# One Trainium2 core, a two-layer hybrid decoder trunk: group A's weights in four transfers, memory's products later, the first norm weighted on rows

## The chip, the cores and the metric

The kernel runs on one core of a Trainium2 chip. The core has TensorE (PE), VectorE (DVE), ScalarE (ACT), GpSimd (POOL) and SyncE (SP), which here only issues transfers. The metric is the device time of one execution in microseconds; lower is better. Times are compared as medians of several executions on the same chip.

## The reference, cut to what matters

The trunk has two layers over 256 tokens of width 1024, in fp32. Each layer normalises the tokens, projects them once, feeds five groups of heads, and projects their outputs back:

```python
for layer in range(DEPTH):
    h = rms_norm(x, pre_norm[layer])
    proj = jnp.einsum('bsd,de->bse', h, w_in[layer])          # 1024 x 8224
    (a_q, a_kv, a_gate, a_z, b_xbc, b_dt, b_z, c_q, c_kv, c_z,
     d_q, d_kv, d_z, m_q, m_z) = jnp.split(proj, offsets, axis=-1)
    a_out = nsa_mixer(...)         # A: compressed, selected and window branches, gated
    b_out = ssd_mixer(...)         # B: conv, Mamba-2 scan; dt = softplus(dt_raw + dt_bias)
    c_out, _ = banded_attention(rope(c_q), rope(c_k), ...)    # C: window 128, sinks
    d_out = dilated_mixer(...)     # D: three dilated windows
    m_out = memory_attention(m_q, mem, m_norm[layer], m_w_kv[layer])   # M: 256 memory tokens
    mix = jnp.concatenate([a_out * silu(a_z), b_out, c_out * silu(c_z),
                           d_out * silu(d_z), m_out * silu(m_z)], axis=-1)
    x = x + rms_norm(jnp.einsum('bse,ed->bsd', mix, w_out[layer]), post_norm[layer])
```

`rms_norm(x, w)` is `x * rsqrt(mean(x*x) + eps) * w`. `rms_norm(mem, m_norm)` is projected to keys and values inside `memory_attention`.

## The kernel before, in words

**Products in three parts.** fp32 accuracy is made from rounded operands: a weight block is loaded into a raw buffer R (`w_load`), rounded into H by a copy on ScalarE or VectorE, and the remainder is put into L by a subtraction on VectorE (`w_split`). The tokens, normalised and transposed, are kept in `hT_hi` and `hT_lo`. A product is then hi x hi, hi x lo and lo x hi. `fm` makes 128 output columns as feature rows for all 256 tokens from one load of 512 KB and 24 matmuls; `tm` makes token rows, by blocks of the contracted dimension (`ks`), 48 matmuls. There are five R buffers, four H and four L, 48 pages of 128x544 (P), and eight PSUM banks (B).

**Order.** Nothing runs as it is called. Every operation is recorded with its engines and estimated costs (`add`), and gets a key: the sum of the PE costs recorded so far plus an offset. `schedule` then simulates the engines: an engine that is free takes the ready operation with the lowest key. The order it finds is the program; each engine executes its own list in order, and semaphores hold the data dependences. The model's times are not waited for, only its order counts. Constants shape the keys: weight loads are due `DMA_EARLY` ahead of their products, splits `W_EARLY` ahead, attention units recorded by `bg` are due `BG_LATE` after, the two norms at the layers' edges are `URGENT`. A load by `dma` goes to SP's queue, at 450 ns of SP in the model; only rounded copies from elsewhere go to POOL's.

**Head (`setup`, `norm_transpose`).** PE first runs `N_WARM` filler products of a page of ones. SP loads the tokens in four parts, the constants (with the identity for transposes) and the norm weights, 32 rows of 128, which PE transposes to per-partition scalars `nw`. For each token tile t, ScalarE sums squares, VectorE makes the inverse root in small steps (`rsqrt`: a bit trick and three Newton steps of two operations), and the rows are scaled. PE transposes them; for each of eight 128-column blocks one operation multiplies by `nw` into `hT_hi` and one VectorE operation multiplies again and subtracts into `hT_lo`. The same function normalises memory (for both layers at once, with the second layer's result stored to DRAM) and the tokens of layer 1.

**Layer (`layer`).** In layer 0 memory's own query and gate products come first (`m_own`); then group A's two compressed key/value products, a `tm` of 288 columns (A's values, A's gates and B's `dt` columns, from three places of the weight, in blocks of 3, 3 and 2 of the eight 128-row blocks: nine transfers), `gates` (A's gates and B's step sizes: softplus of dt by a series, on 128x16 tiles), memory's key/value products and attention units (`m_rest`, `mem_kv`), A's remaining keys with the eight compression pieces, the queries and units of A; then D, B, C and the output products. The rope tables (`setup_rope`: a chain on VectorE and one sine on ScalarE) are recorded at the start with a key `ROPE_LATE` later. In the output products `LAST` of the 18 row blocks are held back, so that they can be done for the first token tile and then the second; the post-norm of the first tile then overlaps the second's products.

## Time and profile before

| | |
|---|---|
| median of 3 runs | 676.24 us (673.43 to 677.6) |
| profiled execution, its own time | 677.86 us |
| its span, first to last instruction | 676.1 us |
| mean granted TensorE clock | 0.991 |
| PE, DVE, ACT, POOL busy in the span | 658.2, 593.4, 474.1, 23.4 us |
| moved by DMA | 125.84 MB, mean 186 GB/s |

The span leaves out what lies around the first and the last instruction, 1.8 us here. Busy times of engines overlap. In the rows below, "L457 MATMUL" is the helper `mm`, "L463" the transpose, "L469" every ScalarE activation, "L486", "L491" and "L511" VectorE's two-tensor, one-tensor and fused operations, "L537" every DMA; tile names stand with their buffer numbers left out.

### The profile page before, as it was taken

Reading aid. Unit: us, or ns where it says so; the run is one execution under the profiler, and the core shown is the slowest. Engines: PE = TensorE matmul, PEld = TensorE weight load, DVE = VectorE, ACT = ScalarE, POOL = GpSimd, SP = SyncE. Lnnn points to the kernel's source line nnn. Section 1 sums busy time; section 2 is a strip of 40 time slices with the busy share of each in tenths; the row PEclk is TensorE's granted clock in tenths of the full one; section 3 lists DMA queues with packets and bytes.
Section 4 is the critical chain, followed back from the end, with each engine's and each line's share of the span. In section 5 each row is a group of like instructions: output and inputs, shape, how many; then the busy total and the mean of one; then the engine's idle time right before and its main releaser. Section 6 shows DMA issues by size and latency. Waiting matters only on the chain.

```text
span 676.1 us, 14725 instructions
## 1 busy us (share of the span) xinstructions
PE 658.2 (97%) x5043; PEld 625.7 (93%) x5043; DVE 593.4 (88%) x1754; ACT 474.1 (70%) x1180; POOL 23.4 (3%) x74
## 2 busy tenths in 40 slices
PE   8989998999999999999999999999999999999995
PEld 7979998999999999988889999999999999998884
DVE  6777989999978999989787879999898899998875
ACT  6663879996765878665475458998576677868541
POOL 3000000000000200100000000000000000000000
PEclk9979998999999999999999999999999999999999
DMA  7899574589998757664438958487989734776511
GB/s 212 226 298 293 164 187 112 153 218 244 236 247 212 185 146 217 184 196 143 158 108 224 258 135 213 104 224 197 237 213 245 199 87 120 208 211 176 156 36 62
DMA packets 177618, 125.84 MB, mean 186 GB/s; under 512 B 11510, under 2 KB 168840, under 8 KB 177544
## 3 DMA queue, kind: packets, MB, share of 16 engines
q1 hardware_dynamic: 176392, 122.81, 67.9%
q0 software_dynamic: 1152, 2.10, 1.2%
q8 instruction: 40, 0.66, 0.4%
q14 instruction: 34, 0.28, 0.1%
HBM read 110.14 MB, written 3.20 MB: 168 GB/s over the span
## 4 chain that ended last, share of the span: by engine, by line
PE 67%; DVE 14%; ACT 7%; DMA 5%; SPq 4%; issue 2%; DVEq 0%; ACTq 0%
PE B L457 64%; ACT P L469 6%; DVE P L486 4%; SPq L537 4%; DMA R<-in_w_in_dram 3%; PE B L463 3%; DVE L L486 3%; DVE P L511 2%; DVE P L515 2%; DVE S L511 1%; DMA P<-in_mem_dram 1%; ACT H L469 1%; DVE P L491 1%; DMA P<-scr 1%; DVE x L511 0%
## 5 line engine op out<-in xcount | busy, mean ns | idle before, releaser
L486 DVE TENSOR_TENSOR L<-R,H 128x1024 fp32r<-128x1024 f32 (+1 forms) x174 | 209.8, 1210 | 33.9 <-ACT H L469 30.9
L469 ACT ACTIVATE H<-R 128x1024 fp32r<-128x1024 f32 (+2 forms) x156 | 163.3, 1055 | 77.5 <-PE B L457 48.8
L469 ACT ACTIVATE P<-B 64x256 f32<-64x256 f32 (+10 forms) x364 | 143.7, 408 | 65.1 <-PE B L457 46.9
L469 ACT ACTIVATE P<-P,S 128x128 f32<-128x128 f32 (+5 forms) x256 | 111.3, 453 | 33.9 <-DVE S L524 17.1
L457 PE MATMUL B<-hT_hi,L 128*128 128x256 f32 x864 | 128.3, 285 | 3.3 <-DVE L L486 3.2
L457 PE MATMUL B<-P,P 128*128 128x256 f32 (+6 forms) x896 | 125.2, 280 | 0.4 <-ACT P L469 0.2
L457 PE MATMUL B<-hT_hi,H 128*128 128x256 f32 x864 | 123.8, 282 | 1.0 <-ACT H L469 1.0
L457 PE MATMUL B<-hT_lo,H 128*128 128x256 f32 x864 | 124.0, 282 | 0.0
L457 PEld LDWEIGHTS B<-P,P 128*128 128x128 f32 (+1 forms) x896 | 113.4, 184 | 3.7 <-DVE P L486 0.9
L457 PEld LDWEIGHTS B<-hT_hi,L 128*128 128x128 f32 x864 | 112.3, 190 | 4.2 <-DVE L L486 3.8
L457 PEld LDWEIGHTS B<-hT_hi,H 128*128 128x128 f32 x864 | 110.9, 188 | 2.3 <-ACT H L469 1.3
L457 PEld LDWEIGHTS B<-hT_lo,H 128*128 128x128 f32 x864 | 110.5, 188 | 0.2
L457 PE MATMUL B<-H,P 128*128 128x512 f32 (+1 forms) x352 | 102.8, 376 | 0.0
L486 DVE TENSOR_TENSOR P<-B,P 64x256 f32<-64x256 f32 (+5 forms) x186 | 92.3, 510 | 11.2 <-ACT P L469 8.8
L457 PEld LDWEIGHTS B<-H,P 128*128 128x128 f32 x352 | 62.1, 189 | 9.6
L457 PE MATMUL B<-L,P 128*128 128x512 f32 (+1 forms) x176 | 65.7, 373 | 0.0
L515 DVE CUSTOM_DVE_ANT_0 P<-B,P 128x128 f32<-128x128 f32 (+2 forms) x192 | 53.1, 320 | 0.4
L463 PE MATMUL B<-cst,P 128*128 128x128 f32 (+1 forms) x344 | 48.5, 275 | 1.2 <-DVE P L491 1.0
L457 PE MATMUL B<-H,hT_hi 128*128 128x256 f32 (+1 forms) x160 | 45.8, 286 | 0.0
L457 PE MATMUL B<-H,hT_lo 128*128 128x256 f32 (+1 forms) x160 | 45.4, 284 | 0.0
L457 PE MATMUL B<-L,hT_hi 128*128 128x256 f32 (+1 forms) x160 | 45.3, 283 | 0.0
L463 PEld LDWEIGHTS B<-cst,P 128*128 128x128 f32 (+1 forms) x344 | 38.4, 136 | 5.7 <-DVE P L491 1.4
(127 smaller groups left out, 665.1 us busy)
## 6 DMA issues: line engine op xcount, KB each, us to landing
R<-in_w_in_dram SPq DMA_DIRECT2D x124, 512.0 KB, 5.4
R<-in_w_out_dram SPq DMA_DIRECT2D x36, 512.0 KB, 3.9
P<-P SPq DMA_DIRECT2D x176, 64.0 KB, 3.9
P<-scr SPq DMA_DIRECT2D x64, 136.0 KB, 4.5
R<-in_m_w_kv_dram SPq DMA_DIRECT2D x8, 512.0 KB, 5.2
P<-in_a_cmp_w_dram SPq DMA_DIRECT2D x16, 256.0 KB, 5.3
mem_d<-P SPq DMA_DIRECT2D x8, 256.0 KB, 5.6
P<-mem_d POOLq DMA_DIRECT2D x8, 256.0 KB, 4.6
```

The costliest lines, as they stand in the source:

```text
L457: f = lambda: self.nc.tensor.matmul(out=out.ap(), lhsT=lhsT.ap(), rhs=rhs.ap(), start=start, stop=stop)
L463: f = lambda: self.nc.tensor.transpose(out.ap(), in_.ap(), idn.ap())
L469: f = lambda: self.nc.scalar.activation(out=out.ap(), in_=in_.ap(), func=func, **{k: _ap(x) for k, x in kw.items()})
L486: f = lambda: self.nc.vector.tensor_tensor(out=out.ap(), in0=a.ap(), in1=b.ap(), op=op)
L491: return lambda: eng.tensor_scalar(out.ap(), a.ap(), _ap(s1), _ap(s2), **kw)
L511: f = lambda: self.nc.vector.scalar_tensor_tensor(out=out.ap(), in0=a.ap(), scalar=_ap(s), in1=b.ap(), op0=op0, op1=op1)
L515: f = lambda: self.nc.vector.tensor_tensor_reduce(out=out.ap(), in0=a.ap(), in1=b.ap(), scale=1.0, scalar=3e38, op0=OP.add, op1=OP.min, ac ...
L537: f = lambda: eng.dma_start(out=_ap(out), in_=_ap(in_))
```

## The change

It does these things:

- The first norm of layer 0 is a new function, `norm_x`. The weight row is loaded into a zeroed buffer, and two fp32 products with a matrix of ones spread it over all partitions in PSUM. For the first token tile the rows are multiplied by the weight and later by the inverse root, for the second both at once. Each of four 512-column pieces is transposed into a bank of its own and split by two 512-wide operations.
- The constants are loaded in two parts, the identity first; the per-partition norm weights, now wanted by memory and layer 1 only, come later.
- Group A's `tm` has 280 columns from two places in blocks of 4 and 4: four transfers; R, H and L grow to 1120 columns. B's `dt` columns are loaded with the neighbouring first half of B's z (264 columns), and the step sizes are computed by `steps`, recorded in B. B's z products now come ahead of its x products.
- `m_rest` of layer 0 is recorded after A's remaining keys and six compression pieces, and memory's load and norm are due 12 instead of 6 us ahead of it.
- The model: SP has eight transfers in flight and costs 520 ns a turn, a PE operation is planned 800 ns after a result of another engine that it uses. Constants: `ROPE_LATE` 80 to 120 us, `LAST` 3 to 4, `N_WARM` 34 to 16 and others.
- `rsqrt` of one column has five steps instead of six.

```diff
...
 TW = 272
+WIDE = 1120
...
 N_RAW, N_HI, N_PAGES, N_SMALL = 5, 4, 48, 64
-SP_HORIZON = 30000.0
-HORIZON, BG_LATE, URGENT, ROPE, LAST = 80000.0, 15000.0, 20000.0, 8000.0, 3
+SP_HORIZON = 40000.0
+HORIZON, BG_LATE, URGENT, ROPE, LAST = 80000.0, 12000.0, 20000.0, 8000.0, 4
...
-KEEP = {"P": (4, 8), "B": (1, 3)}
-LAT = 130.0
+KEEP = {"P": (6, 12), "B": (1, 3)}
+LAT, READ_AHEAD = 130.0, 800.0
...
-DMA_RATE = 250.0
-W_EARLY, DMA_EARLY, T_EARLY, ALT_LATE = 3000.0, 11000.0, 2000.0, 4000.0
+DMA_RATE, DMA_LANES = 250.0, 8
+W_EARLY, DMA_EARLY, T_EARLY, ALT_LATE = 3000.0, 13000.0, 0.0, 2000.0
...
-ROPE_LATE, MEM0_EARLY = 80000.0, 6000.0
-SOME_LATE, PE_LATE, BIAS_LATE = 40000.0, 6000.0, 3000.0
-RESERVE, MEM_EARLY = 1.0, 17000.0
-N_WARM, W_KEY = 34, 0.0
+ROPE_LATE, MEM0_EARLY = 120000.0, 12000.0
+SOME_LATE, PE_LATE, BIAS_LATE = 20000.0, 6000.0, 12000.0
+RESERVE, MEM_EARLY = 1.0, 25000.0
+NR_KEY = -15000.0
+N_WARM, W_KEY = 16, 0.0
...
                         lat = (0.0 if pe and "PE" in alts else 197.0 if pe else LAT) if w else 20.0
+                        if "PE" in alts and not pe:
+                            lat += READ_AHEAD
                         preds[e] = max(preds.get(e, 0.0), lat)
...
     seq = 0
-    dma_clk = 0.0
+    dma_clk, lanes = 0.0, deque()
     now = 0.0
...
                 pe_end = now + cost
+            if op.nbytes and e == "SP":
+                if len(lanes) == DMA_LANES:
+                    cost += max(0.0, lanes.popleft() + 60.0 - now)
             busy[e] = op
...
                 op.t1 = dma_clk + 800.0
+                if e == "SP":
+                    lanes.append(op.t1)
             else:
...
         w = list(writes) + ([out] if isinstance(out, V) else [])
-        self.add({"SP": (450.0, f)} if eng is self.nc.sync else {"POOL": (1000.0, f)}, r, w, nbytes=n)
+        self.add({"SP": (520.0, f)} if eng is self.nc.sync else {"POOL": (1000.0, f)}, r, w, nbytes=n)
...
         self.ts(y.bitcast(I32), v.bitcast(I32), -0.5, OP.mult, float(0x5F3759DF), OP.add)
+        if n == 1:
+
+            h2 = self.small(1)
+            self.ts(h, v, -0.75, OP.mult)
+            self.ts(h2, v, -0.5 / 2.25, OP.mult)
+            self.stt(t, y, h, y, OP.mult, OP.mult)
+            self.stt(y, t, 2.25, y, OP.add, OP.mult)
+            self.stt(t, y, h2, y, OP.mult, OP.mult)
+            self.stt(t, t, 5.0 / 3.0, t, OP.add, OP.mult)
+            self.stt(y, t, 1.25, y, OP.add, OP.mult)
+            return y
         self.ts(h, v, -0.5, OP.mult)
         for _ in range(3):
-            if n == 1:
-                self.stt(t, y, h, y, OP.mult, OP.mult)
-            else:
-                self.tt(t, y, y, OP.mult)
-                self.tt(t, t, h, OP.mult)
+            self.tt(t, y, y, OP.mult)
+            self.tt(t, t, h, OP.mult)
             self.stt(y, t, 1.5, y, OP.add, OP.mult)
...
+    def norm_x(self):
+
+        nwb = self.nwb
+        rows = [[self.page()[:, 0:512] for _ in range(2)] for _ in range(2)]
+        x = lambda t, j: self.x[:, t, 512 * j:512 * j + 512]
+        w = lambda j: nwb[j][:, 0:512]
+        for j in range(2):
+            self.tt(rows[0][j], x(0, j), w(j), OP.mult)
+        rs = [self.inv_rms(self.sum_sq(lambda j: x(t, j))) for t in range(2)]
+        for t in range(2):
+            for j in range(2):
+                if t == 0:
+                    self.scale(rows[t][j], rows[t][j], rs[t], "ACT")
+                else:
+                    self.stt(rows[t][j], x(t, j), rs[t], w(j), OP.mult, OP.mult)
+        parts = []
+        for t in range(2):
+            for j in range(2):
+                b = self.bank()
+                self.begin_fuse()
+                for k in range(4):
+                    self.tr(b[:, 128 * k:128 * k + 128], rows[t][j][:, 128 * k:128 * k + 128])
+                self.end_fuse()
+                d = lambda h: h[:, 4 * j:4 * j + 4, 128 * t:128 * t + 128]
+                v = b.cut(0, k=4, n=128)
+                self.cast(d(self.hi), v)
+                parts.append((d(self.lo), v, d(self.hi).bitcast(F32)))
+        for lo, v, hi in parts:
+            self.tt(lo, v, hi, OP.subtract)
+
...
         self.offset = -9e4
-        self.dma(self.cst.v, self.cin[:, 0:C_OH])
+        self.dma(self.cst[:, 0:C_TRI], self.cin[:, 0:C_TRI])
         self.ident = self.cst[:, C_ID:C_ID + 128]
...
         nr = self.fixed([32, 128], name="nr")
+        row = self.new("R")
+        self.offset = -1.2e5
+        self.zero(row.v)
+        self.ones = self.fixed([128, 128], name="ones")
+        self.zero(self.ones.v, 1.0)
+        self.offset = -1.1e5
+        self.dma(row[0:1, 0:DM], ins["pre_norm"][0:1, :])
+        self.offset = -9e4
+        self.nwb, at = [self.bank() for _ in range(2)], self.pe_time
+        for j in range(2):
+            self.mm(self.nwb[j][:, 0:512], self.ones.v, row[:, 512 * j:512 * j + 512])
+        self.pe_time = at
         self.offset = -1e5
...
         self.offset = -9e4
+        self.dma(self.cst[:, C_TRI:C_OH], self.cin[:, C_TRI:C_OH])
+        self.offset = NR_KEY
         for i, n in enumerate(("pre_norm", "m_norm")):
...
         self.offset = ROPE_LATE
         self.setup_rope()
-        self.offset = -8e4
+        self.offset = NR_KEY + 1e3
         b = self.bank()
...
         gt = self.fixed([128, 2, 24], name=f"gt{l}").v
+        for t in range(2):
+            self.act(gt[:, t], bs[t][:, 256:280], AF.Exp, scale=-1.0)
+        self.ts(gt, gt, 2.0, OP.mult, 2.0, OP.add)
+        self.recip(gt)
+        self.gt = gt
+
+    def steps(self, l, bs):
+
...
-            self.tt(dt[:, t], bs[t][:, 280:288], self.vec[:, l, 0, :], OP.add)
-        self.ts(gt, gt, 2.0, OP.mult, 2.0, OP.add)
-        self.recip(gt)
-        self.gt = gt
+            self.tt(dt[:, t], bs[t][:, 0:8], self.vec[:, l, 0, :], OP.add)
         d = dt.rearrange("p a b -> p (a b)")
...
         kh, kl = self.k_pages(528)
-        bs = self.tm(h, col(A_KV + 384), col(A_KV + 640, 152), col(B_DT, 8), ks=(3, 3, 2))
+        bs = self.tm(h, col(A_KV + 384), col(A_KV + 640, 152))
         av = self.ev_v(bs)
...
         bg(self.gates, l, bs)
-        if l == 0:
-            m_rest(*own)
         cb = self.bank()
...
             piece(), piece()
+        if l == 0:
+            m_rest(*own)
         qs = [self.ev_q(self.fm(h, col(A_Q)))]
...
+        zz = [self.page() for _ in range(2)]
+        for g in range(2):
+            bs = self.tm(h, col(B_Z + 256, 256) if g else col(B_DT, 264))
+            for t in range(2):
+                self.ev_z(bs[t][:, 0:256] if g else bs[t][:, 8:264], zz[t][:, 256 * g:256 * g + 256])
+            if g == 0:
+                bg(self.steps, l, bs)
         pre = bg(self.ssd_pre, l)
...
             XY.append(bg(self.conv, raw, pre[1], i))
-        zz = [self.page() for _ in range(2)]
-        for g in range(2):
-            bs = self.tm(h, col(B_Z + 256 * g, 256))
-            for t in range(2):
-                self.ev_z(bs[t], zz[t][:, 256 * g:256 * g + 256])
         bg(self.ssd, l, pre, XY, zz)
...
             self.offset = -URGENT
-            self.norm_transpose(lambda t, j: self.x[:, t, 512 * j:512 * j + 512],
-                                (self.nw[:, 0, l], lambda k: self.hi[:, k, :], lambda k: self.lo[:, k, :]))
+            if l == 0:
+                self.norm_x()
+            else:
+                self.norm_transpose(lambda t, j: self.x[:, t, 512 * j:512 * j + 512],
+                                    (self.nw[:, 0, l], lambda k: self.hi[:, k, :], lambda k: self.lo[:, k, :]))
             self.offset = 0.0
...
```

## Rows read from the trace of the kernel before

**Rows 1.** The page: busy time, share of the span and instructions of each engine.

```profile
PE 658.2 (97%) x5043; PEld 625.7 (93%) x5043; DVE 593.4 (88%) x1754; ACT 474.1 (70%) x1180; POOL 23.4 (3%) x74
```

**Rows 2.** Windows A:B: length, busy time by engine, granted clock, DMA share, GB/s.

```profile
39.00:43.30 4.30, 1.79 (x10) 1.30 (x8) 4.26 (x10) 4.30 (x12) 0.00 (x0) 0.86 1.14 308
43.30:52.00 8.70, 8.70 (x48) 7.41 (x48) 5.92 (x14) 5.42 (x14) 0.53 (x1) 0.68 1.10 352
52.00:100.00 48.00, 47.59 (x408) 47.16 (x408) 42.38 (x136) 30.21 (x75) 1.08 (x2) 1.00 0.78 210
100.00:104.10 4.10, 1.31 (x12) 1.10 (x10) 3.08 (x10) 4.06 (x13) 0.00 (x0) 0.93 0.39 97
104.10:108.00 3.90, 3.89 (x22) 3.82 (x23) 3.18 (x26) 3.90 (x13) 0.00 (x0) 0.64 0.53 137
108.00:340.00 232.00, 231.53 (x1780) 220.18 (x1778) 214.27 (x614) 168.93 (x424) 11.38 (x33) 1.00 0.72 193
340.00:668.24 328.24, 326.26 (x2518) 310.43 (x2517) 289.14 (x856) 232.41 (x585) 3.64 (x11) 1.00 0.66 171
668.24:676.10 7.86, 0.00 (x0) 0.00 (x0) 4.51 (x14) 0.72 (x3) 0.00 (x0) 0.84 0.36 133
```

**Rows 3.** Timeline, 0 to 16 us: start, length, engine, line, operation, idle before.

```profile
1.35 7.01 PE L457 MATMUL B<-P 128*128 128x512 f32 x23 [1.35 <-POOL P L530]
...
5.18 0.16 DVE L511 SCALAR_TENSOR_TENSOR S<-S 128x1 f32<-128x1 f32 x1 [5.18 <-ACT P L469]
...
5.62 1.31 DVE L511 SCALAR_TENSOR_TENSOR S<-S,S 128x1 f32<-128x1 f32 x6
...
10.56 1.04 PE L463 MATMUL B<-cst,P 128*128 128x128 f32 x8
...
12.30 3.23 DVE L511 SCALAR_TENSOR_TENSOR hT_lo<-B,nw,hT_hi 128x256 fp32r<-128x256 f32 x8 [0.15 <-ACT hT_hi L469]
...
14.75 2.15 PE L457 MATMUL B<-hT_hi,H 128*128 128x256 f32 x16 [0.56 <-ACT H L469]
```

**Rows 4.** DMA issues of one source: size, us from issue to landing.

```profile
nr<-in_pre_norm_dram SPq DMA_DIRECT2D x1, 8.0 KB, 4.0
```

**Rows 5.** Timeline of PE, 39 to 45 us.

```profile
42.15 1.22 PE L457 MATMUL B<-P,H 128*128 128x256 f32 x4 [2.50 <-DVE P L511]
43.30 1.54 PE L457 MATMUL B<-P,rb 32*33 32x400 f32 x2
```

**Rows 6.** Windows, as Rows 2, of four other stretches.

```profile
28.00:36.00 8.00, 8.00 (x68) 8.00 (x67) 3.77 (x7) 3.29 (x7) 0.52 (x1) 1.00 0.45 104
36.00:66.00 30.00, 27.50 (x197) 25.50 (x196) 24.57 (x66) 16.95 (x40) 1.23 (x4) 0.89 1.09 314
148.00:176.00 28.00, 28.00 (x242) 27.84 (x241) 26.67 (x73) 21.69 (x47) 0.83 (x4) 1.00 0.95 247
224.00:262.00 38.00, 37.80 (x313) 36.81 (x313) 37.82 (x82) 32.99 (x77) 4.89 (x10) 1.00 0.70 186
```

**Rows 7.** Timeline, 98 to 105 us: the sine and what waits.

```profile
99.01 1.28 ACT L469 ACT_TABLE_LOAD   x1
...
100.31 0.63 ACT L469 ACTIVATE sincos<-P 128x512 f32<-128x512 f32 x1
100.96 1.28 ACT L469 ACT_TABLE_LOAD   x1
100.98 0.35 DVE L491 TENSOR_SCALAR sincos<-sincos,cst 128x256 f32<-128x256 f32 x1 [1.34 <-ACT sincos L469]
...
104.11 1.22 PE L457 MATMUL B<-hT_hi,L 128*128 128x256 f32 x4 [2.80 <-DVE L L486]
```

**Rows 8.** Timeline of DVE, 59 to 63 us: end of the step sizes' chain.

```profile
62.36 0.17 DVE L491 TENSOR_SCALAR dt<-dt 128x16 f32<-128x16 f32 x1
```

**Rows 9.** Timeline of the end.

```profile
667.31 1.42 DVE L511 SCALAR_TENSOR_TENSOR x<-P,S,x 128x512 f32<-128x512 f32 x2
...
668.64 1.28 DVE L486 TENSOR_TENSOR P<-B,N 128x512 f32<-128x512 f32 x2
```

More of the change, by code (lines that the diff above doesn't have):

```diff
@@ L416, in __init__ @@
         ctx.enter_context(tc.manual_schedule())
-        self.slots = {"P": N_PAGES, "B": 8, "R": N_RAW, "H": N_HI, "L": N_HI, "S": N_SMALL, "N": 2}
-        self.dims = {"P": PGW, "B": 512, "R": 1024, "H": 1024, "L": 1024, "S": 16, "N": DM}
+        self.slots = {"P": N_PAGES, "B": 8, "R": N_RAW, "H": N_HI, "L": N_HI, "S": N_SMALL, "N": 1}
+        self.dims = {"P": PGW, "B": 512, "R": WIDE, "H": WIDE, "L": WIDE, "S": 16, "N": DM}
     @contextmanager
@@ L762, in setup @@
         self.zero(self.acsT.v)
-        self.ones = self.fixed([128, 128], name="ones")
-        self.zero(self.ones.v, 1.0)
         self.offset = ROPE_LATE
         self.setup_rope()
-        self.offset = -8e4
+        self.offset = NR_KEY + 1e3
         b = self.bank()
@@ L910, in gates @@
         for t in range(2):
-            self.act(gt[:, t], bs[t][:, 256:280], AF.Exp, scale=-1.0)
-            self.tt(dt[:, t], bs[t][:, 280:288], self.vec[:, l, 0, :], OP.add)
-        self.ts(gt, gt, 2.0, OP.mult, 2.0, OP.add)
-        self.recip(gt)
-        self.gt = gt
+            self.tt(dt[:, t], bs[t][:, 0:8], self.vec[:, l, 0, :], OP.add)
         d = dt.rearrange("p a b -> p (a b)")
@@ L1523, in layer @@
         for n, k in enumerate(WO_ORDER):
-            ws.append(self.w_split(self.w_load((lambda r: r.v, ins["w_out"][l][128 * k:128 * k + 128, :]))))
+            ws.append(self.w_split(self.w_load((lambda r: r[:, 0:DM], ins["w_out"][l][128 * k:128 * k + 128, :]))))
             if n < 18 - LAST:
```

## The prediction, made before the change was run

> **What bounds the kernel now.** I read the page first: TensorE (PE) is busy 658.2 of 676.1 us, VectorE (DVE) 593.4, ScalarE 474.1 [rows 1]. With PE at 97% the question is not which engine is fastest to relieve but where PE's missing time lies: idle time, half-clock time, and the time before it has useful work. The windows by stage answer that. From 108 to 340 us PE idles 0.47 us and from 340 to 668 us 1.98 us; from 52 to 100 it is 0.41 [rows 2]. Nothing in the steady body is worth a per cent. The time to win is in four places. (a) The head: the first long run of real products starts at 14.75 us [rows 3]; until then PE runs filler on constants. (b) 39 to 52 us: 2.51 us idle, then the granted clock is 0.86 and 0.68 [rows 2]. At two levels, 1.2 and 2.4 GHz, a mean of 0.68 over 8.7 us is 5.6 us at the lower one, half of it lost: 2.8; the 1.15 us of work between 42.15 and 43.3 lost another 0.6. Stage price 5.9. PE waited for the memory's low halves on DVE [rows 5]. (c) 100 to 108 us: 2.79 us idle, then 0.64 over 3.9 us, 1.4 lost: 4.2 in all. The timeline shows why: ScalarE loads a table, does the rope's sine, loads the table back, 3.2 us together; DVE stands behind it in order for 1.34 us, and the weights' low half comes late to PE [rows 7]. (d) The tail, 7.86 us after PE's last product [rows 2].
>
> So the ceiling of any reordering is about 5.9 + 4.2 + 2.9 (all other idle) plus what the head and tail give.
>
> **The change, part by part.**
>
> *Head.* Before, the first norm scales rows, transposes both token tiles and applies the weight as a per-partition scalar after, in eight 256-wide pairs; the eight low halves alone take 3.23 us [rows 3]. After, the weight is spread over partitions by two fp32 products with ones, multiplied in on rows, and hi and lo are four 512-wide operations each. DVE's work up to the rows: a statistics chain of 1.75 us, from 5.18 to the end of the six [rows 3], becomes some 0.1 shorter; two of them, two products from PSUM at 0.64 and two scalings at 0.71 [rows 9] make 3.3 + 1.3 + 1.4 = 6.0, so 11.2 us if nothing is waited for. The weight row is new: its nearest transfer, another norm row, lands 4.0 us after issue [rows 4]; leaving SP between x's transfers near 2.5 us, it lands near 6.5. On SP it waits for POOL's zeros, with x's last part, the constants and all weight loads queued behind it; on DVE the two products wait for it, with the second statistics chain and the low halves behind. A fp32 product of 400 columns took 1.54 us at the lower clock [rows 5], so 512 columns take 1.0 to 2.0, two end at 8.5 to 10.4, and the second token tile's rows at 10.6 to 12.5. I take 11.5. Four transposes (0.5 of eight's 1.04 [rows 3]) and a 512-wide copy (0.63, as the sine's [rows 7]) follow; the first half of the columns is earlier, so steady products start near 12.3. Before, it was 14.75 less the eight products already done at 0.13 (2.15/16), 13.7. Gain 1.4, bounds -1.4 (below) to +2.5. On SP the first weight load goes out two turns later (the row, the second part of the constants); what PE waited for at 14.75 was not a landing but a weight's high copy on ScalarE [rows 3], queued behind the norm's copies there, of which there are now fewer, so the two turns are hidden. If that cover is gone they cost about 1 us.
>
> *Memory's products later (layer 0).* Between group A's products and memory's own now stand two K products and six compress pieces. Moved with them: four loads of memory, sixteen transposes, 32 norm operations, eight stores and four key/value weight loads on SP; their due time moves with the products but twice as far ahead, so loads and norms move about 5 us and products about 11. Where PE stood for 2.51 us, it has those other products if their weights have landed. SP and the DMA engines decide that: from 28 to 36 us they moved 104 GB/s, from 36 to 66 us 314 GB/s at a full share [rows 6]. Filling the first of these brings some 8 x 0.2 = 1.6 MB forward, enough for three weight loads of 0.5 MB. Group A's three-part loads, among them 8-column ones, become four with fewer SP turns; the 8 columns move to the z load, 288 to 280 and 256 to 264 columns, so PE's work is equal. I take 3.7 of the 5.9, bounds 0 and 5.9.
>
> *The sine later.* Its key goes from 80 to 120 us of product time, past unit A's last work and ahead of the first dilated unit, some 150 to 170 us here. The eleven DVE operations, the position load and the same 3.2 us of ScalarE go with it. From 148 to 176 ScalarE is busy 21.7 of 28 us [rows 6], against all of 100 to 104 [rows 2], so a delay is made good in a few us rather than handed on; DVE is at 26.7 of 28, so its 1.3 us wait is only partly covered. I take 2.3 of the 4.2, bounds -1 and 4.2. The Trainium skill speaks against this: "ScalarE: Activation LUTs", What ACT_TABLE_LOAD costs, adds a drain of about 1.38 us to each load's 1.28. By that figure the block would be some 2.8 us longer, and the gain an estimated zero. The trace disagrees: the sine starts 0.02 us after the first load ends, and the row's price stands.
>
> *Planner's model.* PE operations on fresh non-PE results are planned 0.8 us later, and SP is modelled with eight transfers in flight. Neither adds a wait; both change the order. Of the 2.9 us of small idles I take 0.9 back, bounds -4 and 2.9.
>
> *Step sizes to group B.* The 24 small DVE operations at 0.17 us [rows 8], 4 us a layer, leave a stage in which DVE has room (24.6 of 30 [rows 6]) for one where it is busy 37.8 of 38, 224 to 262 us [rows 6]. What hides the chain is the second z and the eight x products recorded behind it, 240 matmuls or 31 us at the mean of 0.13 (1780 in 231.5 us [rows 2]); I take -0.7 in all, bounds 0 and -8.
>
> *Tail.* Holding four instead of three products back frees the first token tile's chain 1.4 us earlier (six matmuls of 512 columns, an estimate from 2.4 GHz and gaps). Its last operation now ends at 668.73, on top of the second tile's first at 668.64 [rows 9]; about 0.25 comes back, and 0.1 from the shorter inverse root. 0.35.
>
> Sum: 1.4 + 3.7 + 2.3 + 0.9 - 0.7 + 0.35 = 7.95. The profiled execution took 677.86 us (span 676.1 and 1.8 around it), giving 669.9; it is 1.6 above the median of the runs, 676.24, against which I predict: 668.3.
>
> **The rivals.** *The stalls only move* (no change, 674). The DMA engines are full from 36 to 66 us [rows 6], so PE, sent on to K and compress, waits there for weights; the sine hands its 3.2 us on in its new place, since DVE has 1.3 us of room in 28. Then only head, tail and half of the small idles remain: 1.4 + 0.35 + 0.5 = 2.2. Against it: 1.6 MB of unused transfer time just before.
>
> *The step sizes stall group B in both layers* (slower, 684). With DVE full, the chain of 24 waits behind splits and conv work; cumulative sums, decays and the scan wait for it, and products find no free PSUM bank. Each layer then pays the chain's 4 us and a stall like the sine's, 4.2: 16.4 over the forecast without this term, 667.6. It decides once the chain starts so late that PE has used up the z and x products, the 31 us above. Against: that cover is long.
>
> *The row of weights is late and the filler short* (672). Filler falls from 34 products to 16, and on POOL the row's zeros now come ahead of the filler's page; 23 of them lasted 7.0 us from 1.35 [rows 3], so 16 end near 8 to 9, and PE is thinly used until 12. If the clock falls as it did after 104 us, 1.4 is lost instead of won: 668.3 + 2.8 = 671.1, with 1 us for the late row 672.
>
> *Everything goes* (663): head 2.5, both stalls whole, 10.1, small idle 0.5, tail 0.35: 13.4.
>
> **How the numbers follow.** Forecast, 665 to 672: 0.47. Stalls move: 0.21. Late row: 0.09. Everything: 0.15. Step sizes: 0.08. About 1%, 6.8 us, is what a measurement here can tell from no change: faster means under 669.5, slower over 683. Two thirds of the forecast case and all of "everything" are faster: 0.47; slower is 0.08; the rest, 0.45, is the same. The range 662.5 to 677 leaves out the slower rival and the far ends of others.
>
> **What would show it.** Steady products from about 12.3 us with the clock at full; no PE idle over 1 us and no clock below 0.9 between 36 and 56 us; table loads near 150 to 170 us with no PE wait of over 1 us behind them; the last x update starting near 0.35 us sooner after PE's end. Wrong if PE waits on weight loads between 36 and 60, if a half-clock stretch appears in the head, or if DVE-released PE waits show up in group B around 220 and 545 us.

## The result, and the profile after

The changed kernel takes 672.83 us, median of 20 runs (670.39 to 678.69), the kernel before 676.89 in 20 runs beside it: a ratio of 0.9949, 95% interval 0.9931 to 0.9967. That is about 3.4 us (0.0051 x 676) where 8 were forecast; the two medians lie 4.1 apart, and the ratio, which uses all runs, is what is compared here. Below, a ratio's difference of 0.001 is 0.68 us.

The page of the changed kernel, the line of busy times, to be read against [rows 1]:

```profile
PE 652.2 (97%) x5029; PEld 621.5 (92%) x5029; DVE 594.0 (88%) x1753; ACT 472.0 (70%) x1171; POOL 24.7 (4%) x75
```

Its windows (length, busy time by engine, granted clock, DMA share, GB/s), to be read against [rows 2]:

```profile
0.00:14.50 14.50, 10.01 (x38) 6.84 (x38) 8.66 (x29) 9.08 (x17) 6.94 (x25) 1.00 0.81 231
14.50:36.00 21.50, 21.50 (x178) 21.30 (x179) 13.09 (x21) 9.09 (x17) 0.00 (x0) 1.00 0.81 206
36.00:56.00 20.00, 17.10 (x136) 16.83 (x134) 18.02 (x54) 15.71 (x36) 1.71 (x5) 0.91 1.10 314
56.00:90.00 34.00, 34.00 (x285) 33.00 (x285) 29.40 (x68) 20.64 (x51) 0.52 (x1) 1.00 0.87 240
90.00:130.00 40.00, 40.00 (x341) 39.64 (x340) 39.59 (x185) 38.77 (x138) 0.52 (x1) 1.00 0.64 160
130.00:190.00 60.00, 57.64 (x482) 56.11 (x481) 55.77 (x167) 47.29 (x102) 1.02 (x6) 1.00 0.77 186
190.00:336.00 146.00, 146.00 (x1064) 136.67 (x1063) 132.07 (x363) 100.38 (x232) 10.07 (x24) 1.00 0.70 195
336.00:366.00 30.00, 27.73 (x203) 25.73 (x202) 27.31 (x76) 22.91 (x48) 1.72 (x5) 1.00 0.74 204
366.00:664.65 298.65, 298.26 (x2321) 285.36 (x2320) 266.08 (x783) 207.41 (x535) 2.18 (x8) 1.00 0.64 170
664.65:672.00 7.35, 0.00 (x1) 0.00 (x0) 4.03 (x13) 0.72 (x3) 0.00 (x0) 0.80 0.24 89
```

The same windows of before where the stages of [rows 2] are cut otherwise:

```profile
36.00:56.00 20.00, 17.50 (x111) 15.50 (x110) 16.48 (x37) 14.48 (x35) 1.23 (x4) 0.83 1.11 332
90.00:130.00 40.00, 36.98 (x297) 36.07 (x296) 36.81 (x157) 37.21 (x115) 0.63 (x2) 0.96 0.66 170
...
336.00:366.00 30.00, 29.03 (x200) 26.19 (x199) 25.27 (x70) 22.21 (x49) 1.57 (x3) 1.00 0.51 134
```

A window's price is its idle time plus PE's busy time by what the clock lacks. Between 36 and 56 us before lost 2.50 + 17.50 x 0.17 = 5.5, after 2.90 + 17.10 x 0.09 = 4.4. Around the sine before lost 3.0 + 1.5 = 4.5 at 90 to 130; after loses nothing there but 2.36 at 130 to 190, against 0.05. The layer boundary, 336 to 366, went the wrong way, from 0.97 to 2.27. The tail [rows 2] fell from 7.86 to 7.35. Group B, inside 190 to 336, doesn't idle at all.

The head, from the timeline of the changed kernel (start, length, engine, line, operation, idle before):

```profile
10.13 1.40 DVE L520 SCALAR_TENSOR_TENSOR P<-x,S,B 128x512 f32<-128x512 f32 x2
...
10.83 1.06 ACT L478 ACTIVATE H<-R 128x1024 fp32r<-128x1024 f32 x1 [0.25 <-DMA R<-in_w_in_dram]
...
11.80 0.58 ACT L478 ACTIVATE hT_hi<-B 128x512 fp32r<-128x512 f32 x1
11.93 1.23 DVE L495 TENSOR_TENSOR L<-R,H 128x1024 fp32r<-128x1024 f32 x1 [0.26 <-ACT H L478]
...
12.60 1.06 ACT L478 ACTIVATE H<-R 128x1024 fp32r<-128x1024 f32 x1 [0.22 <-DMA R<-in_w_in_dram]
...
13.57 1.07 ACT L478 ACTIVATE hT_hi<-B 128x512 fp32r<-128x512 f32 x2
```

The rows of both token tiles are ready at 11.53, as forecast (11.5). But on ScalarE two weight splits (10.83 and 12.60) stand among the high copies, on DVE one at 11.93, and the last copies run at 13.57. PE starts steadily at 14.50, having waited 2.02 us; forecast was 12.3. Group A's first product comes at 31.49 us against 30.82 in before, with the same six groups ahead of it.

The memory stage, SyncE's and PE's timelines of the changed kernel:

```profile
21.46 2.35 SPq L546 DMA_DIRECT2D P<-P  x2
...
24.53 5.50 SPq L546 DMA_DIRECT2D P<-P  x6
30.07 1.23 SPq L546 DMA_DIRECT2D R<-in_w_in_dram  x2
31.35 2.22 SPq L546 DMA_DIRECT2D P<-in_mem_dram  x3
```

```profile
41.27 1.97 PE L472 MATMUL B<-cst,P 128*128 128x128 f32 x8 [2.90 <-DVE P L500]
42.89 1.90 PE L466 MATMUL B<-hT_hi,H 128*128 128x256 f32 x8
```

PE waits 2.90 us for memory's transposes, not for products, and the products of K that were to fill the gap stand behind them at 42.89. Memory's rows were late because three of its four loads left SyncE at 31.35; ScalarE, which sums their squares, had one of them at 37.27:

```profile
37.27 0.63 ACT L478 ACTIVATE P<-P 128x512 f32<-128x512 f32 x1 [0.16 <-DMA P<-in_mem_dram]
```

SyncE had spent 24.53 to 30.03 on six `P<-P` transfers of 64 KB, the swaps of memory's query halves. What it waited for between 24.5 and 30.05 us (us in total, times, longest):

```profile
SPq L546 <- DMA R<-in_w_in_dram: 2.0, 3, 0.7
```

These three waits are for the landing of weight loads: the program uses eight semaphores in turn for SyncE's transfers, and in the trace each of the three swaps waits for the transfer issued eight before it. The rest of the 5.50 us is mostly the issuing itself, 0.46 to 0.70 us a swap. No wait for the evictions that write the query halves shows in this stretch; one of 0.8 us, for ScalarE, came earlier, at 21.46.

The sine's block after [rows 7], ScalarE's timeline:

```profile
149.93 1.28 ACT L478 ACT_TABLE_LOAD   x1
151.22 0.63 ACT L478 ACTIVATE sincos<-P 128x512 f32<-128x512 f32 x1
...
156.50 1.28 ACT L478 ACT_TABLE_LOAD   x1 [1.70 <-DVE S L533]
```

The second table load now comes 4.7 us behind the sine, before the next exponential; in before it followed at once.

### The profile page after: what moved, and what is told of

Its sections match the earlier page's. It is cut to its first block, busy times and chain, and to the rows that moved or that the text cites. A ratio compares the mean times of both kernels' runs of the same rounds, so it can differ in the third digit from the quotient of the medians.

```text
span 672.0 us, 14666 instructions
## 1 busy us (share of the span) xinstructions
PE 652.2 (97%) x5029; PEld 621.5 (92%) x5029; DVE 594.0 (88%) x1753; ACT 472.0 (70%) x1171; POOL 24.7 (4%) x75
## 4 chain that ended last, share of the span: by engine, by line
PE 71%; DVE 11%; DMA 7%; ACT 6%; SPq 2%; issue 2%; DVEq 0%; ACTq 0%
PE B L466 67%; DMA R<-in_w_in_dram 4%; PE B L472 4%; ACT P L478 4%; DVE P L495 3%; SPq L546 2%; DVE L L495 2%; DVE P L524 2%; ACT H L478 2%; DMA P<-P 1%; DMA vec<-in_b_d_dram 1%; DVE S L520 1%; DMA x<-in_x_dram 1%; DVE P L500 1%; DVE P L520 0%
## 5 line engine op out<-in xcount | busy, mean ns | idle before, releaser
L495 DVE TENSOR_TENSOR L<-R,H 128x1024 fp32r<-128x1024 f32 (+2 forms) x172 | 209.7, 1224 | 32.3 <-ACT H L478 28.7
L478 ACT ACTIVATE H<-R 128x1024 fp32r<-128x1024 f32 (+1 forms) x151 | 159.3, 1059 | 73.1 <-PE B L466 33.1
L478 ACT ACTIVATE P<-B 64x256 f32<-64x256 f32 (+10 forms) x346 | 137.6, 410 | 61.4 <-PE B L466 43.8
L478 ACT ACTIVATE P<-P,S 128x256 f32<-128x256 f32 (+5 forms) x268 | 116.0, 453 | 29.3 <-DVE S L533 11.5
L466 PE MATMUL B<-P,P 128*128 128x256 f32 (+6 forms) x896 | 127.3, 278 | 2.0 <-DVE P L520 1.9
L466 PE MATMUL B<-hT_hi,H 128*128 128x256 f32 x864 | 125.7, 284 | 2.0 <-DVE hT_hi L559 2.0
L466 PE MATMUL B<-hT_hi,L 128*128 128x256 f32 x864 | 126.1, 283 | 0.0
L466 PE MATMUL B<-H,hT_hi 128*128 128x256 f32 (+2 forms) x160 | 46.1, 288 | 0.0
L466 PE MATMUL B<-L,hT_hi 128*128 128x256 f32 (+2 forms) x160 | 45.5, 284 | 0.0
L466 PE MATMUL B<-H,hT_lo 128*128 128x256 f32 (+2 forms) x160 | 45.3, 283 | 0.0
```

What stands on the lines that cost most here:

```text
L466: f = lambda: self.nc.tensor.matmul(out=out.ap(), lhsT=lhsT.ap(), rhs=rhs.ap(), start=start, stop=stop)
L478: f = lambda: self.nc.scalar.activation(out=out.ap(), in_=in_.ap(), func=func, **{k: _ap(x) for k, x in kw.items()})
L495: f = lambda: self.nc.vector.tensor_tensor(out=out.ap(), in0=a.ap(), in1=b.ap(), op=op)
```

## Experiments

Ratios are against before on the same chip. Single windows are read as above.

**What a new order costs by itself.** The planner writes all five instruction lists anew after any edit. Two runs change one constant by 1 ns; e1 in the changed kernel.

```diff
-LAT, READ_AHEAD = 130.0, 800.0
+LAT, READ_AHEAD = 131.0, 800.0
```

> The changed kernel with one planning constant moved by a hair (a result is taken as readable 131 ns after its operation, not 130). Nothing of the work differs; the planner writes the five instruction lists anew from the first few products on. It sizes what a new order alone does. If the places of the change matter and not the luck of an order: 0.995 +- 0.0015 of the kernel before, 672.8 +- 1 us, the idle time at the layer boundary (about 340 to 362 us) near 2.3 us. If orders differ by luck by as much as the change is worth: over 2 us from 672.8 either way, and boundary idle anywhere from 0.3 to 4 us.

Measured 675.73 us, ratio 0.9990 (0.9968 to 1.0012): 2.8 us of the 3.4 are gone with no work changed (by the two intervals, 0.9 to 4.7).

e5 does the same in before (`LAT` 130 to 131):

> The kernel before, with the same constant moved by a hair as in the re-planned changed kernel (131 ns in place of 130); nothing of the work differs. If the order of before is an ordinary one among its neighbours: within 1 us of before (0.9985 to 1.0015), and the change's real worth is its re-planned neighbour's 0.999, some 1 us or nothing. If before's own order was a lucky or an unlucky one: more than 2 us from it, either side, and then the measured 0.995 says little of the change itself.

676.11 us, 0.9998 (0.9976 to 1.0021): by this one neighbour, before's order is an ordinary one. So part of the measured gain belongs to one order of the changed kernel, and differences under some 2 us between single variants prove little.

**The memory stage.** e2 undoes the move: `m_rest` recorded ahead of A's keys again, with a lead of 6 us.

```diff
-ROPE_LATE, MEM0_EARLY = 120000.0, 12000.0
+ROPE_LATE, MEM0_EARLY = 120000.0, 6000.0
...
+        if l == 0:
+            m_rest(*own)
         cb = self.bank()
...
-        if l == 0:
-            m_rest(*own)
         qs = [self.ev_q(self.fm(h, col(A_Q)))]
```

> Memory's products of layer 0 recorded where they were before the change, with the old lead of 6 us for their loads; all else as changed. If the move is what the shorter stall between 38 and 48 us comes from, as the prediction had it (worth 3.7), the stage returns to 5.9 us lost, 1.3 more than the 4.6 lost in the changed kernel, and the total to about 674 us; if the forecast's whole term was only masked by something else, up to 676.5. Rival: the planner places memory's transposes and products when their rows are ready in its own model, and in its list TensorE's first 170 rows or so are the same with either place, so the move itself does nothing: 2.9 us idle near 38 to 41 us again, lost time within 0.4 us of 4.6, total within 1 us of 672.8.

675.57 us, 0.9987 (0.9964 to 1.0009). Its windows:

```profile
36.00:56.00 20.00, 16.52 (x103) 14.42 (x102) 19.31 (x54) 14.79 (x34) 1.19 (x4) 0.83 1.10 308
```

It lost 3.48 + 16.52 x 0.17 = 6.3 in the stage, 1.9 more than the changed kernel. The rival's statement that the lists agree was wrong (memory's products run from 45.06 here, ahead of K); the move changes the order. Whether it gains is not shown, for e5, with no work changed, differs from before's 5.5 in this stage by as much, with 1.95 + 18.05 x 0.09 = 3.6:

```profile
36.00:56.00 20.00, 18.05 (x128) 16.79 (x127) 17.38 (x39) 15.23 (x36) 1.19 (x4) 0.91 1.09 324
```

In the total, too, e2 is where the re-planned e1 is.

e3 puts K first: loads as in the change, memory's norm due 16 us later.

```diff
-ROPE_LATE, MEM0_EARLY = 120000.0, 12000.0
+ROPE_LATE, MEM0_EARLY, NORM_EARLY = 120000.0, 16000.0, -4000.0
...
+            self.offset += MEM0_EARLY - NORM_EARLY
             every = [out] + [pages() for _ in range(1, self.depth)]
```

> The loads of memory keep their due time, but the norm and the transposes of memory fall due after the two K products (16 us later), so that in TensorE's list the 48 matmuls of K and half of the compress products stand ahead of memory's transposes. If the order of TensorE's list is what kept the stall alive: no idle time over 1 us between 35 and 44 us, the clock at 0.95 or more there, 3 to 4 us less than the changed kernel, 669 to 670. If data is the limit (weights of K or memory's own rows late, the DMA engines full): the wait moves to K's weights at 38 us or to memory's transposes and high halves some 6 us later, 2 to 3 us idle in another place, total 672 to 674.

674.51 us, 0.9982 (0.9960 to 1.0004). K's products run at 38.29 and 39.34, as meant, and then:

```profile
42.88 1.98 PE L466 MATMUL B<-P,P 128*128 128x48 f32 x16 [2.43 <-DVE S L520]
```

The compressor's operands are late in place of memory's: 2.43 us. PE's list was not the limit; what the list waits for moved. So e7 lets the swaps fall due 25 us later (`Q_LATE`):

```diff
-                self.dma(q[64 * i:64 * i + 64, par].bitcast(F32), ...)
+                with self.later(Q_LATE if self.fresh and not self.units else 0.0):
+                    self.dma(q[64 * i:64 * i + 64, par].bitcast(F32), ...)
```

> The changed kernel, with the eight transfers that swap the halves of memory's queries falling due 25 us later. They wait for evictions, and SyncE stood behind six of them for 5.5 us with three of memory's loads and K's weights queued behind it. If the transfer queue's order is what makes memory's rows late: memory's loads are issued by 26 us in place of 31 to 33.6, TensorE's wait for memory's transposes near 41 us falls from 2.9 to under 0.8 us, the clock stays up, 3 to 4 us less over 35 to 50 us, total 669 to 670.5. If the DMA engines' rate is the limit (they show a full share from 36 us): loads issued sooner land little sooner, the wait stays over 2 us, total within 1 us of 673 to 675.

669.52 us, 0.9912 (0.9881 to 0.9943). SyncE's timeline, and PE's:

```profile
24.46 2.09 SPq L546 DMA_DIRECT2D P<-in_mem_dram  x2
...
27.07 1.44 SPq L546 DMA_DIRECT2D P<-in_mem_dram  x1
...
33.40 3.56 SPq L546 DMA_DIRECT2D P<-P  x4
```

```profile
39.43 1.09 PE L472 MATMUL B<-cst,P 128*128 128x128 f32 x8 [1.04 <-DVE P L500]
```

Memory's three loads leave 6 to 7 us sooner, the wait falls to 1.04, the clock holds, and the gain grows from 3.4 to 6.0 us. The expectation's "They wait for evictions" is not what held SyncE: four swaps take 3.56 us at 33.40 as well, and no wait shows there. What mattered is that their turns in the queue came ahead of memory's loads. e8 has K first on top of it (both diffs above):

> The same late swaps, and K's products ahead of memory's transposes as in the earlier run that put K first. If list order and queue order both held the stage, this frees it most: no idle time over 0.7 us between 35 and 52 us, the clock at 0.97 or more, total 668.5 to 670.5. If the rate of the DMA engines is the limit, TensorE waits 1.5 to 2.5 us for the compressor's weights or for memory's rows at 40 to 50 us, total 673 to 675.

669.92 us, 0.9911 (0.9884 to 0.9938): no more than late swaps alone; the wait of 1.1 us moves to 53.5 us. e9 has late swaps in before, with nothing of the change:

> The kernel before, with memory's query swaps due 25 us later and nothing of the change. In before the loads of memory and group A's weights were issued ahead of the swaps, so only memory's key and value weights and the compressor's stood behind them. If the swaps alone held the stage in both kernels: its 5.9 us shrink to under 2, total 671 to 673, and the changed kernel's parts are worth little beyond it. If before was held by memory's norm on DVE (TensorE waited for its low halves): the 2.5 us wait near 40 us stays, total within 1.5 us of before.

673.51 us, 0.9956 (0.9933 to 0.9979), as much as the whole change. Its windows:

```profile
36.00:56.00 20.00, 20.00 (x158) 18.80 (x157) 19.59 (x48) 13.93 (x34) 1.19 (x4) 1.00 1.08 329
90.00:130.00 40.00, 37.38 (x301) 36.34 (x300) 36.51 (x163) 37.95 (x126) 0.74 (x3) 0.96 0.65 163
```

The stage that lost 5.5 us loses none, although the edit leaves memory's norm as it is; the sine's 4.1 stays. What held the stage in before is in its timeline:

```profile
26.16 4.06 SPq L537 DMA_DIRECT2D P<-P  x6
...
30.27 3.61 SPq L537 DMA_DIRECT2D R<-in_w_in_dram  x4
...
35.66 0.68 ACT L469 ACTIVATE H<-R 128x576 fp32r<-128x576 f32 x1 [2.30 <-DMA R<-in_w_in_dram]
...
36.38 0.76 DVE L486 TENSOR_TENSOR L<-R,H 128x576 fp32r<-128x576 f32 x1 [1.93 <-ACT H L469]
```

Group A's last weights left SyncE behind the eight swaps, which with one load took 24.10 to 30.22 us (0.5 of it a wait for a landing, 1.2 for ScalarE and VectorE). ScalarE waited for them, VectorE for ScalarE, and the norm of memory stands behind this split in VectorE's list; PE's wait of 2.50 us [rows 5] is the end of that chain. The queue held the stage in both kernels.

**The head.** e4 brings the high copies forward, by leaving the 0.8 us out in the first norm:

```diff
-                            lat += READ_AHEAD
+                            lat += 0.0 if op.urgent and self.units == 0 else READ_AHEAD
```

> In the first norm alone TensorE's operations are planned without the added 0.8 us after other engines' results. In ScalarE's list the first high copy of x then stands ahead of both weight splits, and DVE's list changes alike. If the queues' order was what held the first steady products until 14.5 us (rows had been ready at 11.5): products run steadily from 12.7 to 13.3 us and the stages behind shift by as much, 1.2 to 1.8 us off 672.8. If weights or clock held them: steady products from 14.2 to 14.8 us still, total within 0.7 us.

675.38 us, 0.9979 (0.9950 to 1.0009). Steady products start at 12.88, group A at 30.08, 1.4 us sooner; the memory stage then lost 1.30 + 18.70 x 0.17 = 4.5, as in the changed kernel. e11 is the same with late swaps:

> The changed kernel with late swaps, and in the first norm alone no added 0.8 us in TensorE's planning, which put the first high copy ahead of the weight splits and started steady products at 12.85 us in the earlier run, where a stall with a falling clock at 44 us ate it. With that stall gone the head's gain should reach the end: 1.2 to 1.7 us faster than 669.5, 667.8 to 668.4. If each us won in the head is waited away for transfers at 36 to 50 us: within 0.5 us of 669.5.

669.50 us, 0.9900 (0.9872 to 0.9928), 0.8 us by the ratio, nothing by the medians: the head's 1.0 us at group A doesn't show at the end. e10 has before's head on the changed kernel with late swaps (`norm_transpose` for both layers, 34 fillers, one transfer of constants, no weight row):

> The changed kernel with late swaps (669.5 us, its clock never down), and the head of before: rows scaled, transposed, weighted per partition, 34 filler products, one transfer of constants, no row of weights. If the new head costs time, as the windows have it (first steady products at 14.2 to 14.5 against an effective 13.7): 0.5 to 1 us faster, 668.5 to 669. If it gains what the prediction said: 1 to 1.5 us slower, 670.5 to 671.

666.59 us, 0.9858 (0.9828 to 0.9889), 3.7 us faster than with the new head. e17 has the old head alone, swaps as in the change:

> The changed kernel with the head of before and nothing else undone, swaps as in the change. If the new head costs 1 us or more by itself: group A's first product at 30.5 to 30.9 in place of 31.5 us, total 669.5 to 672. If the head's cost was only an order's luck in the earlier run: 672.8 to 675, as the other re-planned neighbours.

668.88 us, 0.9897 (0.9863 to 0.9932), 3.5 us faster than the changed kernel. SyncE's timeline and the stage's window:

```profile
17.59 4.02 SPq L546 DMA_DIRECT2D P<-P  x4
...
23.49 2.38 SPq L546 DMA_DIRECT2D P<-P  x4
...
27.21 2.89 SPq L546 DMA_DIRECT2D P<-in_mem_dram  x4
```

```profile
36.00:56.00 20.00, 19.05 (x156) 17.87 (x155) 19.05 (x55) 14.95 (x37) 1.69 (x5) 1.00 1.04 298
```

Group A starts at 31.05, only 0.4 us sooner. The larger part is the queue again: with this head's order the swaps leave at 17.59 and 23.49, and all four of memory's loads follow at 27.21 instead of 31.35; the stage loses 0.95 instead of 4.4.

**The sine's place.** e6, in the changed kernel:

```diff
-ROPE_LATE, MEM0_EARLY = 120000.0, 12000.0
+ROPE_LATE, MEM0_EARLY = 80000.0, 12000.0
```

> The changed kernel with the rope's due time back at 80 us of product time; TensorE's list is the same up to 48 us and differs behind. If the sine's late place is worth the 2.2 us read from the windows: the block of table load and sine near 100 us stalls TensorE again for some 2.5 to 4 us with the clock falling once, the 2 us idle at 156 to 164 us goes, total 674.5 to 676. If the stalls only move, with the same price in both places: within 1 us of 672.8.

671.84 us, 0.9948 (0.9921 to 0.9975): the same. The old-head kernel with late swaps (666.59) loses nothing at 36 to 56 us and its clock stays up; the next runs change one part of that calm base. Its windows:

```profile
90.00:130.00 40.00, 40.00 (x340) 39.65 (x339) 39.57 (x168) 38.61 (x124) 0.54 (x1) 1.00 0.70 175
130.00:190.00 60.00, 58.94 (x501) 58.03 (x500) 57.04 (x165) 45.09 (x92) 1.19 (x6) 1.00 0.86 213
...
336.00:366.00 30.00, 27.70 (x226) 26.83 (x225) 26.95 (x64) 19.89 (x39) 0.52 (x1) 1.00 0.84 226
```

e13, re-planned only (`LAT` 131):

> The changed kernel with late swaps and the old head (666.6 us), with only the planning constant moved from 130 to 131 ns. If the 3 us that a re-plan cost the changed kernel were the memory stall and its falling clock, there is little to lose here: within 1 us of 666.6. If order alone is worth 3 us anywhere: 665 to 670.

668.07 us, 0.9863 (0.9840 to 0.9886): 0.3 us by the ratio, 1.5 by the medians. e14, the sine at 80 us:

> The same base, the rope's due time at 80 in place of 120 us. If the sine's late place is worth 2.2: 668.5 to 669.5, with a wait of 2.5 us or more near 95 to 110 us. If it stalls TensorE as long in either place, or in neither: within 1 us of 666.6.

666.85 us, 0.9852 (0.9827 to 0.9877): the same. Its windows:

```profile
90.00:130.00 40.00, 38.77 (x321) 37.64 (x320) 37.49 (x154) 36.74 (x113) 0.52 (x1) 1.00 0.61 156
130.00:190.00 60.00, 59.98 (x515) 59.54 (x513) 58.32 (x172) 47.66 (x112) 1.04 (x6) 1.00 0.82 218
```

1.23 us idle in the early place, 1.06 in the late one: the wait moves, its price doesn't change.

**The planner's 0.8 us**, taken away on the calm base (e15):

```diff
-LAT, READ_AHEAD = 130.0, 800.0
+LAT, READ_AHEAD = 130.0, 0.0
```

> The same base, TensorE's operations planned without the added 0.8 us after other engines. If that model doubled the idle time at the layer boundary: idle there falls from 2.3 to about 1 us, and small idles elsewhere grow by at most 1: 665.5 to 666.6. If the model is what keeps the steady body free of idles: boundary unchanged, 2 us or more of new small waits, 668.5 or more.

673.12 us, 0.9923 (0.9903 to 0.9943): 4.4 us slower. Its windows:

```profile
130.00:190.00 60.00, 57.97 (x483) 57.53 (x482) 51.62 (x149) 42.47 (x89) 1.04 (x6) 0.97 0.82 192
190.00:336.00 146.00, 143.58 (x1030) 133.05 (x1029) 131.67 (x361) 99.58 (x231) 9.67 (x24) 1.00 0.71 199
336.00:366.00 30.00, 28.89 (x212) 26.83 (x211) 28.14 (x77) 22.84 (x48) 1.72 (x5) 1.00 0.68 185
```

The boundary is back to 1.11, but 2.42 us are idle at 190 to 336 and 3.8 are lost at 130 to 190. e18 takes it away only for the urgent operations (`0.0 if op.urgent else READ_AHEAD`):

> The changed kernel with late swaps and the old head, and the 0.8 us left out only for the operations of the norms and the layer boundary's chain. If the model of the norm's transposes alone doubled the boundary's idle time: 2.3 falls to 1.0 to 1.3 there, total 665 to 666. If that idle is set by weights' low halves on DVE, planned elsewhere: 2.0 to 2.3 still, total 666 to 668.

666.58 us, 0.9862 (0.9825 to 0.9899). The boundary falls to 1.29 idle, but 3.2 us are lost at 130 to 190 in this execution, and the total is that of the calm base.

**The step sizes**, back in group A with its three-part loads, on the calm base (e16; the z products move back too):

```diff
-        bs = self.tm(h, col(A_KV + 384), col(A_KV + 640, 152))
+        bs = self.tm(h, col(A_KV + 384), col(A_KV + 640, 152), col(B_DT, 8), ks=(3, 3, 2))
...
         self.gt = gt
+        self.steps(l, bs)
```

> The same base, with the step sizes back in group A: its loads in three parts of three transfers, 8 columns of their own, the 24 small DVE operations behind the gates, the second z after the x products. If the move is free, as its place without a stall in group B says: within 1 us of 666.6. If the three-part loads with their extra transfers cost the stage at 30 to 45 us, as the prediction counted in the move's favour: 1 to 3 us slower, with waits for group A's weights. If the move cost the 0.7 predicted: 665.9.

671.90 us, 0.9914 (0.9890 to 0.9937): 3.8 us slower, with 2.39 us idle at 36 to 56 and 2.75 at the boundary. The move gains, together with the four wider loads that came with it.

**Three products held back** in place of four, with late swaps (e12, `LAST` 4 to 3):

> The changed kernel with late swaps, three products of the output held back in place of four. All runs of the changed kernel and its variants idle 2.0 to 2.4 us at the layer boundary (340 to 362), before 0.5 to 1.0. If holding four back is what makes weights late there: idle falls to about 1 us, the tail after the last product grows by 0.3 to 0.4, total 0.8 to 1 us faster, 668.5. If not: boundary idle 2 us or more still, total 669.5 to 670.

672.69 us, 0.9944 (0.9921 to 0.9968), 2.2 us slower than with four. The boundary is worse (3.33 idle), not better; from PE's end to the last x update it takes 2.89 us, as with four.

## Why the prediction was off: the direction right, most of its steps wrong

The direction held, and the time lies in the range, but above the forecast case (665 to 672). Four of the six terms were mis-sized, two of them in sign, and a fifth came out for another reason; that the total is in the range is in part luck, since terms that came out too low stand against terms that came out too high. Two rivals name nearly this time, 674 and 672. Of the first, the stalls that only move, the sine bears out its part; in the memory stage PE waited for memory's rows, not for the weights that it names. The late row of weights is not what happened: the rows were ready in time and the clock was 1.00 up to 14.5 us.

- **Head, +1.4 forecast, a loss measured.** The step that failed is that four transposes and "a 512-wide copy" follow on the rows without a wait: the rows came when forecast, but the copies stood behind weight splits in ScalarE's and DVE's lists. The prediction had seen this queue from the other side only, weights behind the norm's copies. With the first copy ahead (e4) steady products start at 12.88, near the forecast 12.3. Group A starts 0.7 us later than in before. The old head gives 3.5 and 3.7 us in two pairs of kernels, most of the first by its queue order. What the second's rest is made of stays open: 2.0 of it are waits (36 to 56 and 130 to 190), and the head fixed in place gave nothing sure.
- **Memory, +3.7 forecast, 1.1 in the stage, less than a new order alone makes there (1.9 between before and e5).** "Filling the first of these brings some 8 x 0.2 = 1.6 MB forward" failed: the 104 GB/s of [rows 6] were no free capacity. SyncE issues in order, and there it was busy with the small swaps and then for 3.61 us with four pieces of group A's weights; the change put three of memory's four loads behind the swaps. The wait for DVE [rows 5] named the last link only; in e9 the whole stage's loss is gone with the norm as it was. Of the eleven kernels with late swaps ten lose at most 1.4 us in this stage, at full clock, and e16, with the old loads of group A, 2.4. Of the nine without, e17 loses 0.95, its swaps having left earlier; the others lose 3.6 to 8.6. The Trainium skill ("DMA: Bandwidth & Descriptors", Issuing engines are not separate DMA queues) calls the issuing engine's time "usually small relative to the DMA itself"; for one swap the trace agrees (0.46 to 0.70 us, and 2.0 to 5.8 to its landing), but six in a row held SyncE 5.50 us, their waits included.
- **Sine, +2.3 forecast, 2.2 read from the windows, yet not for the reason given.** The step that failed is that a delay is "made good" in the new place: PE still idles 2.36 us there, 1.85 of it in one wait that ends at 160.77. The place is worth nothing in two pairs (e6, e14); there the stalls only move, as the rival said. In the old place e6 idles 2.62 us and e14 1.23, against before's loss of 4.5; what took the rest off is another part of the change or its order, and was not tried in before. On the drain that the Trainium skill adds to a table load ("ScalarE: Activation LUTs", What ACT_TABLE_LOAD costs) the trace disagrees again: the sine starts at 151.22, 0.01 us after the load's end.
- **Planner's model, +0.9 forecast, about 4.4.** Undoing the 0.8 us costs that much on the calm base. The step that failed is to take this term out of before's 2.9 us of small idles: without the 0.8 us, 3.8 us are lost at 130 to 190 and 2.4 at 190 to 336, where before loses 0.05 and 0.19. It also costs 1.2 at the layer boundary. The other half of the model, eight transfers in flight, was not undone by itself.
- **Step sizes, -0.7 forecast, +3.8.** The cover of 31 us held (190 to 336 is full). The sum counted a cost and put the wider loads at nothing; with the old loads and the chain back, group A's stage and the boundary wait 2.8 us longer. The run undoes columns, loads and chain together, so it doesn't say which.
- **Tail, +0.35 forecast, +0.5.** Right in size, wrong in parts. From PE's end to the last update it takes 2.89 us instead of 3.38, with three held back (e12) as with four, so the fourth adds nothing. The chain of small operations before the update is 0.25 shorter (1.78 to 1.53), where the inverse root was put at 0.1, and VectorE is free for the second tile 0.06 us after PE's end instead of 0.40, with three held back too. That the shorter root is behind both is not shown, since no run has the six steps back.

These prices overlap, since one stall hides another, and don't add up to 3.4. The order's luck, up to 3 us here, stood nowhere in the sum; the range held it.

The fastest version is the changed kernel with late swaps and the old head, 666.6 us, 1.4% below before.

## What to carry to other kernels

Before counting a stretch of low DMA traffic as room, look at the issuing queue: small transfers take a turn each there, and a wait of one of them holds every load behind it. The wait that PE shows is named after the last engine of that chain; follow it back from engine to engine. Where a planner orders the work, run an edit of nothing first; a gain of its size is not yet the edit's. Undo each part on a kernel without the big stall, since beside one the parts hide behind each other.

## What was not expected of the hardware

The price of one stall differs between executions. With the sine early (e6, the same TensorE list as in the changed kernel up to 86 us), the profiled execution took 679.21 us at a mean granted clock of 0.988, another 670.92 at 0.998; its windows show where:

```profile
36.00:56.00 20.00, 17.22 (x98) 16.95 (x96) 15.92 (x50) 13.71 (x33) 1.19 (x4) 0.66 0.97 268
```

A wait of 2.8 us was followed by 5.9 us of lost clock (17.22 x 0.34), where the changed kernel's profile, with a wait of 2.9 us in the same place, lost 1.5. Of 35 runs of before, the 12 at a clock of 0.990 or less have a median of 678.5, the 9 at 0.996 or more 674.7. Whether late swaps narrow the spread is not shown: e7's six runs span 3.2 us, e12's ten 5.4, these 35 of before 7.8.
